# A two-layer hybrid encoder: the opening, the last pair of each ConvFFN and the ending written out by hand

## The chip, the cores and the metric

The kernel runs on one core of a Trainium2 chip. The metric is the device time of one execution in microseconds, smaller is better.

The core has TensorE (PE, the matrix products, with its weight loads as PEld), VectorE (DVE), ScalarE (ACT), GpSimd (POOL) and SyncE (SP). Each runs its own queue of instructions in order. SyncE issues DMAs; GpSimd can issue them too, from its own queue, among its other instructions.

## The reference

The kernel computes one step of a two-layer encoder on 1024 prompt frames and 32 frames of a running stream, with 1024 channels:

```
rmsnorm(x, g) = x * rsqrt(mean(x*x) + 1e-6) * g

layer 0:  gb, gc, u = split(rmsnorm(x, a_norm) @ w_in, 3)     # short gated conv
          x = x + (gb * causal_conv3(gc * u)) @ w_out
          x = x + conv_ffn(rmsnorm(x, ffn_norm[0]))
shared:   k, v, forget = rmsnorm(x, kv_norm) @ w_kv
layer 1:  q = rmsnorm(x, b_norm) @ w_q
          x = x + forgetting_attention(q, k, v, forget) @ w_o
          x = x + conv_ffn(rmsnorm(x, ffn_norm[1]))
y = rmsnorm(x, final_norm)

conv_ffn(h):  g, v = split(causal_conv3(h @ w_up), 2)         # 2 x 2816 channels
              return (silu(g) * v) @ w_down
```

The output is y and the new states (the last two rows of each convolution, K, V and the forget logits).

## The kernel before

All activations are kept with channels on partitions. The stream x is eight tiles of 128 channels by 1056 tokens (1024 and 32), x0 to x7. The token axis is cut in three chunks of 352 (`CH`), in two halves of 528 (`HALVES`), or, before a norm, in four chunks of 264 (`ENDS`). A product of float32 numbers is made of three products of a rounded type: each operand is split into a high part (ScalarE copies it into the rounded type) and a low part (VectorE subtracts the high part from the number), and `chain` (L259, L260, L261) adds high by high, low by high and high by low in one bank of PSUM. A weight tile goes the same way: `weights` (L222) loads it raw by SyncE, ScalarE makes wh (L236) and VectorE wl (L237). A unit is the product of all of x with 128 output channels: eight blocks, three chunks and three products, so 72 products.

The order of instructions in each queue is set by a scheduler with a model of times. Where code runs under `strict` (L102), the instructions of TensorE, VectorE and ScalarE keep the order in which they are written, and all are recorded with line 73; SyncE and GpSimd go by the scheduler there too.

**The opening.** `build` loads the eight tiles of x and two weight tiles. `normed` splits each tile, times its gain, into xh (L248) and xl (L249), and squares it on ScalarE (L314); the squares are added to acc by GpSimd, the last by VectorE (L315). The first units do not wait for the statistics of the norm: `start(acc, 2)` makes the first two (gc and u of the mixer) go through `outer`, block by block, and `settle` multiplies their results later by the scale. The scale comes from `rstd`: 24 small products of acc with ones (L359), the square root on ScalarE, a Newton step on VectorE, a diagonal dg, and products of dg with ones (L332) that spread the scale over the partitions. The third unit (gb) goes the usual way, behind the scale.

**The end of ConvFFN.** `ffn` runs over 22 pairs of units g and v. For each pair it puts the two rows of state in front of a sample's tokens (`halo`, L483, GpSimd), copies the last rows out (`tail`, L487, GpSimd), makes the three taps (the first on ScalarE, L497, two on VectorE, L501), silu, product and split (L832, L833). While these loops run, x lies in DRAM; behind them SyncE loads its eight tiles again, 16 DMAs of 128x528 (L165). Then come the last four activations of w_down: in layer 0 by `down`, with weight tiles by `weights`; in layer 1 by blocks of 512 columns (L716, L723, L724) and `tokenwise`.

**The ending.** In layer 1 `tokenwise` goes chunk by chunk of 264 tokens and row by row (m = 0 to 7): 12 products for a row, VectorE adds them to x, ScalarE squares, VectorE adds the square to acc. `tick` moves a counter on by one row, and `at(n, f)` puts f that many rows later. In the first chunk all rows get their first three activations ahead of the last one. The statistics of a chunk stand in the next one (`rstd_steps`). `result` (L455) writes the output of a chunk behind its scale: ScalarE x * gain, GpSimd that times the scale (L468), DMA (L469); in the last chunk VectorE makes six rows at once from x, gain and scale, and ScalarE with GpSimd two.

The tiles x and y lie in a pool of 24 buffers (`keep`), weight tiles in one of four, raw weights in one.

## Time and profile before

| what | us |
|---|---|
| timed runs | 2527.67, 2531.79, 2531.83 |
| their median | 2531.79 |
| the profiled execution | 2527.23 |
| its span, from first to last instruction | 2525.40 |
| busy in it: TensorE | 2462.6 (98%) |
| VectorE | 1525.6 (60%) |
| ScalarE | 1213.8 (48%) |
| GpSimd | 898.5 (36%) |

The profile is of one execution. Its times count from the start of the span. TensorE's granted clock is given as a share of full speed; the mean over the span is 0.994. A row of the timeline gives in brackets how long the engine stood idle ahead of the instruction, and what released it.

### The profile page before, as it was taken

How to read it: one execution, taken by the hardware profiler on the slowest of the kernel's cores; microseconds unless marked ns; L12 is line 12 of the kernel's file. 1: busy time of each engine (PE TensorE's matmuls, PEld its weight loads, DVE VectorE, ACT ScalarE, POOL GpSimd, SP SyncE). 2: the span in 40 equal slices, each digit the busy share in tenths (PEclk: the TensorE clock that was granted, in tenths of full speed). 3: DMA queues.
4: the chain of work that ended last, by engine and by line, in shares of the span. 5: the costliest groups of instructions: out<-in, count | busy, mean ns of one | idle time of the engine just before them, and what ended most of it. 6: DMA issues, size and time to landing. Idle time of an engine off the chain costs nothing. (4 is left out here: it accounts for less than half of the span.)

```text
span 2525.4 us, 47206 instructions
## 1 busy us (share of the span) xinstructions
PE 2462.6 (98%) x18484; PEld 2425.1 (96%) x18484; DVE 1525.6 (60%) x2593; ACT 1213.8 (48%) x2380; POOL 898.5 (36%) x952
## 2 busy tenths in 40 slices
PE   7999999999999999999999999999999999999997
PEld 7999999999999999998999999999999999999996
DVE  6443448855555555666676667665885555555575
ACT  4111114555555545445666666643554555555544
POOL 3000012444444434342544445412244444334423
PEclk9999999999999999999999999999999999999998
DMA  3111123376666666532322223373246766666751
GB/s 120 42 48 45 49 87 93 65 131 120 119 117 111 119 118 120 138 114 65 80 73 76 76 78 81 81 245 102 71 95 119 128 117 119 114 114 116 123 138 69
DMA packets 147631, 254.76 MB, mean 101 GB/s; under 512 B 22352, under 2 KB 58320, under 8 KB 147408
## 3 DMA queue, kind: packets, MB, share of 16 engines
q0 software_dynamic: 41472, 77.88, 23.2%
q1 hardware_dynamic: 105936, 173.87, 22.9%
q8 instruction: 145, 2.38, 0.4%
q14 instruction: 78, 0.64, 0.1%
HBM read 130.52 MB, written 113.04 MB: 96 GB/s over the span
## 5 line engine op out<-in xcount | busy, mean ns | idle before, releaser
L734 PE MATMUL pb_p<-b,wb 128*128 128x264 f32 x6720 | 894.8, 284 | 2.0 <-ACT u L776 2.0
L734 PEld LDWEIGHTS pb_p<-b,wb 128*128 128x128 f32 x6720 | 850.0, 188 | 2.4 <-ACT u L776 2.4
L900 POOL DMA_DIRECT2D xd<-xs x288 | 262.8, 917 | 495.9 <-ACT xs L898 494.5
L898 ACT ACTIVATE xs<-pb_d 128x264 f32<-128x264 f32 x576 | 218.3, 387 | 349.8 <-PE pb_d L261 307.5
L259 PE MATMUL pb_d<-acth,wb 128*128 128x264 f32 x1152 | 327.7, 285 | 1.3 <-ACT xs L898 1.3
L260 PE MATMUL pb_d<-actl,wb 128*128 128x264 f32 x1152 | 327.5, 285 | 0.0
L261 PE MATMUL pb_d<-acth,wb 128*128 128x264 f32 x1152 | 327.3, 285 | 0.0
L259 PE MATMUL pb_d<-xh,wh 128*128 128x384 f32 (+2 forms) x864 | 283.1, 331 | 8.4 <-ACT xh L248 7.5
L260 PE MATMUL pb_d<-xl,wh 128*128 128x384 f32 (+2 forms) x864 | 282.1, 327 | 5.9 <-DVE xl L249 5.8
L261 PE MATMUL pb_d<-xh,wl 128*128 128x384 f32 (+2 forms) x864 | 281.4, 326 | 0.0
L501 DVE SCALAR_TENSOR_TENSOR y<-u,cv,y 128x1058 f32<-128x1058 f32 x186 | 238.9, 1330 | 54.0 <-ACT y L497 53.9
L259 PEld LDWEIGHTS pb_d<-acth,wb 128*128 128x128 f32 x1152 | 216.6, 188 | 2.2 <-ACT xs L898 1.9
L261 PEld LDWEIGHTS pb_d<-acth,wb 128*128 128x128 f32 x1152 | 216.9, 188 | 0.0
L260 PEld LDWEIGHTS pb_d<-actl,wb 128*128 128x128 f32 x1152 | 216.8, 188 | 0.0
L236 ACT ACTIVATE wh<-wraw 128x1024 fp32r<-128x1024 f32 (+1 forms) x69 | 72.3, 1047 | 258.2 <-PE pb_d L260 137.4
L483 POOL COPY u<-cv 128x4 f32<-128x4 f32 x96 | 64.9, 676 | 346.3 <-DVE u L691 248.7
L724 DVE TENSOR_TENSOR wb<-wr,wb 128x512 fp32r<-128x512 f32 x196 | 153.1, 783 | 55.8 <-ACT wb L723 45.5
L724 DVE TENSOR_TENSOR wb<-ws,wb 128x512 fp32r<-128x512 f32 x160 | 125.0, 783 | 98.0 <-ACT wb L723 98.0
L259 PEld LDWEIGHTS pb_d<-xh,wh 128*128 128x128 f32 x864 | 162.7, 189 | 10.0 <-ACT xh L248 8.2
L756 POOL TENSOR_TENSOR ws<-wr 128x512 f32<-128x512 f32 x80 | 122.3, 1528 | 137.0 <-DMA wr<-in_w_up 113.6
L260 PEld LDWEIGHTS pb_d<-xl,wh 128*128 128x128 f32 x864 | 163.1, 189 | 8.0 <-DVE xl L249 7.7
L261 PEld LDWEIGHTS pb_d<-xh,wl 128*128 128x128 f32 x864 | 162.9, 189 | 0.3
(343 smaller groups left out, 4949.8 us busy)
## 6 DMA issues: line engine op xcount, KB each, us to landing
xd<-xs POOLq DMA_DIRECT2D x288, 264.0 KB, 4.3
wr<-in_w_up SPq DMA_DIRECT2D x168, 256.0 KB
wr<-in_w_down SPq DMA_DIRECT2D x80, 256.0 KB
x<-xd SPq DMA_DIRECT2D x48, 264.0 KB
wraw<-in_w_in SPq DMA_DIRECT2D x23, 512.0 KB
xd<-x SPq DMA_DIRECT2D x64, 132.0 KB
wraw<-in_w_kq SPq DMA_DIRECT2D x16, 512.0 KB
xd<-x SPq DMA_DIRECT2D x16, 264.0 KB
```

Source lines behind the costliest of these rows:

```text
L236: nc.scalar.activation(h[:, i:j], raw[:, i:j], AF.Copy)
L259: nc.tensor.matmul(ps, wh, xh[:, c[0]:c[1]], start=(i == 0), stop=False)
L260: nc.tensor.matmul(ps, wh, xl[:, c[0]:c[1]], start=False, stop=False)
L261: nc.tensor.matmul(ps, wl, xh[:, c[0]:c[1]], start=False, stop=(i == n - 1))
L483: self.nc.gpsimd.tensor_copy(v, st.rearrange("p (a b) -> p a b", b=2))
L501: self.nc.vector.scalar_tensor_tensor(y, u[:, i:i + TC], w[:, i:i + 1], y, op0=OP.mult, op1=OP.add)
L724: nc.vector.tensor_sub(t[:, 1], src, t[:, 0].bitcast(F32))
L734: nc.tensor.matmul(ps[:, q, :QB], w[:, i, k], t[:, j, cs], start=(begin and k == 0 and n == 0), stop=(end and k == len(b) - 1 and n == 2), ...
L756: getattr(self.nc.gpsimd, "tensor_" + op)(dst, x, y)
L898: nc.scalar.activation(t[:, q * QB:(q + 1) * QB], ps, AF.Copy)
L900: nc.gpsimd.dma_start(d, t, accum_op=OP.add)
```

## The change

Three functions are written anew, and all that is in them is put in order by hand under `strict`.

`opening` takes the place of the loads in `build`, of `normed`, `start` and `settle` for the first three units. All loads are issued at the start, with the raw weights of the second unit between x3 and x4 and those of the third behind x7, each in a buffer of its own. ScalarE and VectorE split all of x first; the squares (ScalarE) and their sums (VectorE, none on GpSimd) stand behind that, between the products of the second unit. The statistics stand behind the first chunk of the third unit, the products that spread the scale behind its second.

`halved`, in `ffn`, takes the place of `act` for the last pair: both halo copies first, then taps, silu, product and split for the columns up to 528, and then for the rest. The 16 loads of x go to GpSimd's queue, and in layer 0 the weights of `down` get a high priority.

`ending` takes the place of `tokenwise` with `lag` and of `result`. ScalarE writes x * gain into y right behind the square of the same row, in every chunk. The add of a square to acc comes two rows later (one for the last row). Behind the scale GpSimd multiplies rows 0 to 4 and VectorE rows 5 to 7, which reads the scale from PSUM; in the last chunk VectorE takes rows 0 to 5.

At the start of attention some chains of products change places in TensorE's order, with no code of their own changed; the scheduler sets that.

```
     def load(self, x, m, queue=None):
         x[m] = self.keep(f"x{m}")
         for d, cs in self.spilled(m):
-            self.nc.sync.dma_start(x[m][:, cs], d)
+            (queue or self.nc.sync).dma_start(x[m][:, cs], d)
...
+    def ending(self, weight, acts, x):
...
+        def add(ps, m, c, y):
+            cs = slice(*c)
+            xc = x[m][:, cs]
+            self.nc.vector.tensor_add(xc, xc, ps)
+            sq = acc[:, cs] if m == 0 else self.temp("sq")[:, :c[1] - c[0]]
+            self.nc.scalar.activation(sq, xc, AF.Square)
+            self.nc.scalar.activation(y[m // 2][:, m % 2], xc, AF.Copy, scale=self.gain[:, 5, m:m + 1])
+            if m:
+                self.at(1 if m == NK - 1 else 2, lambda: self.nc.vector.tensor_add(acc[:, cs], acc[:, cs], sq))
+
+        def scaled(y, m, c, r):
+            engine, by = (self.nc.gpsimd, out[:, slice(*c)]) if r is None else (self.nc.vector, r)
+            engine.tensor_mul(y[m // 2][:, m % 2], y[m // 2][:, m % 2], by)
...
             for m in range(NK):
+                ps = early[m] if early else next(banks)[:, :n]
+                self.chain(ps, weight(m), acts, c, range(g - 1, g) if early else None)
+                self.tick()
+                self.at(1, lambda ps=ps, m=m, c=c, y=y: add(ps, m, c, y))
...
+        for m in (0, 6, 1, 2, 7, 3, 4, 5):
+            scaled(y, m, c, None if m > 5 else r)
...
-                tiles[i // 8] = self.weights(units[i // 8])
+                with self.tc.high_priority(offset=2 * AHEAD) if lag else nullcontext():
+                    tiles[i // 8] = self.weights(units[i // 8])
...
+    def opening(self, x, gain):
...
+        products(0, range(1))
+        for m in range(1, NK):
+            high(m)
+            low(m)
+            if m == 1:
+                whigh(0, 2)
+                wlow(0, 2)
+            products(0, range(m, m + 1))
+        whigh(1)
+        wlow(1)
+        sq = [self.slot("sq") for _ in range(NK)]
+        for m in range(NK):
+            ACT.activation(sq[m], x[m], AF.Square)
+            if m:
+                DVE.tensor_add(sq[0], sq[0], sq[m])
+            products(1, range(m, m + 1))
+            if m == 1:
+                for i in range(3):
+                    evict(0, i)
+            if m == 4:
+                whigh(2)
+                wlow(2)
...
+        def halved(t, g, v):
...
+            for u, _, i in both:
+                self.halo(u, st[:, i])
...
+            for a, b in ((0, HB), (HB, TC)):
...
-            put_off += act(t, *us)
+            put_off += act(t, *us) if t < NF - 1 else [lambda: halved(t, *us)]
...
         for m in range(NK):
-            self.load(x, m)
+            self.load(x, m, nc.gpsimd)
...
-                self.tokenwise(lambda m: [(ws[m][:, 0, k], ws[m][:, 1, k]) for k in range(4)], acts, x,
-                               self.result(x), lag=True)
+                self.ending(lambda m: [(ws[m][:, 0, k], ws[m][:, 1, k]) for k in range(4)], acts, x)
```

VectorE at the opening, before (wraw is a raw weight tile, wh and wl its parts, x_99 to x_106 the blocks of x, sq a square):

```order
L237 TENSOR_TENSOR wl<-wraw,wh 128x256
L237 TENSOR_TENSOR wl<-wraw,wh 128x768
L249 SCALAR_TENSOR_TENSOR xl<-x_99,gain,xh 128x352 x3
L249 SCALAR_TENSOR_TENSOR xl<-x_100,gain,xh 128x1056
L249 SCALAR_TENSOR_TENSOR xl<-x_101,gain,xh 128x1056
L249 SCALAR_TENSOR_TENSOR xl<-x_102,gain,xh 128x1056
L249 SCALAR_TENSOR_TENSOR xl<-x_103,gain,xh 128x1056
L237 TENSOR_TENSOR wl<-wraw,wh 128x1024
```

The same place after (wr is the raw tile of `opening`):

```order
L73 TENSOR_TENSOR wl<-wr,wh 128x256
L73 SCALAR_TENSOR_TENSOR xl<-x_99,gain,xh 128x352 x3
L73 SCALAR_TENSOR_TENSOR xl<-x_100,gain,xh 128x1056
L73 TENSOR_TENSOR wl<-wr,wh 128x768
L73 SCALAR_TENSOR_TENSOR xl<-x_101,gain,xh 128x1056
L73 SCALAR_TENSOR_TENSOR xl<-x_102,gain,xh 128x1056
L73 SCALAR_TENSOR_TENSOR xl<-x_103,gain,xh 128x1056
L73 SCALAR_TENSOR_TENSOR xl<-x_104,gain,xh 128x1056
L73 SCALAR_TENSOR_TENSOR xl<-x_105,gain,xh 128x1056
L73 SCALAR_TENSOR_TENSOR xl<-x_106,gain,xh 128x1056
L73 TENSOR_TENSOR wl<-wr,wh 128x1024
L73 TENSOR_TENSOR sq<-sq 128x1056
```

The rest of the first weight's low part stands behind block 1 now, the second weight's behind all blocks, and the sums of squares, which GpSimd made beside these rows, follow there on VectorE.

GpSimd at the end of ConvFFN in layer 0, before (u is the output of a unit, cv the states, ws a weight block that GpSimd adds up):

```order
L756 TENSOR_TENSOR ws<-wr,ws 128x512
L483 COPY u<-cv 128x2x2 x2
L487 COPY cv<-u 128x4 x2
L483 COPY u<-cv 128x2x2 x2
L487 COPY cv<-u 128x4
```

The same place after (xd is x in DRAM; the first two and the last two of the 16 loads are shown):

```order
L909 TENSOR_TENSOR ws<-wr,ws 128x512
L512 COPY u<-cv 128x2x2 x2
L516 COPY cv<-u 128x4
L165 DMA x_11708<-xd_69 128x528
L165 DMA x_11708<-xd_70 128x528
...
L165 DMA x_11729<-xd_83 128x528
L165 DMA x_11729<-xd_84 128x528
L516 COPY cv<-u 128x4
L512 COPY u<-cv 128x2x2 x2
L516 COPY cv<-u 128x4
```

The 16 loads stand ahead of the tail copy of the pair before and of the two halo copies of the last pair.

ScalarE in the last chunk of the ending, before (ne is the square root in the statistics, the numbered x are rows 0 to 7):

```order
L73 ACTIVATE sq<-x_28324 128x264
L73 ACTIVATE y<-x_28309,gain 128x264
L73 ACTIVATE y<-x_28312,gain 128x264
L73 ACTIVATE y<-x_28315,gain 128x264
L73 ACTIVATE y<-x_28318,gain 128x264
L73 ACTIVATE y<-x_28321,gain 128x264
L73 ACTIVATE y<-x_28324,gain 128x264
L73 ACTIVATE sq<-x_28327 128x264
L73 ACTIVATE y<-x_28327,gain 128x264
L73 ACTIVATE y<-x_28330,gain 128x264
L73 ACTIVATE sq<-x_28330 128x264
L73 ACTIVATE ne<-pb_d,epst 88x3
```

The same place after:

```order
L73 ACTIVATE sq<-x_28344 128x264
L73 ACTIVATE y<-x_28344,gain 128x264
L73 ACTIVATE sq<-x_28347 128x264
L73 ACTIVATE y<-x_28347,gain 128x264
L73 ACTIVATE sq<-x_28350 128x264
L73 ACTIVATE y<-x_28350,gain 128x264
L73 ACTIVATE sq<-x_28353 128x264
L73 ACTIVATE y<-x_28353,gain 128x264
L73 ACTIVATE ne<-pb_d,epst 88x3
```

Before, six writes of y of the chunk ahead stand between the squares of rows 5 and 6; after, each square is followed by the write of its own row.

## Rows read from the trace of the kernel before

**Rows 1.** Stretches from the span's start, TensorE: us, busy (instructions), clock, DMA share, GB/s.

```profile
0.00:56.77 56.77, 42.64 (x247) 1.00 0.36 124
56.77:350.00 293.23, 293.23 (x1841) 1.00 0.16 47
...
1050.00:1250.00 200.00, 191.22 (x1254) 0.98 0.33 100
...
2448.00:2525.40 77.40, 56.84 (x422) 0.86 0.25 90
```

**Rows 2.** Timeline of the opening: start, us, engine, line, operation, count [idle <-releaser].

```profile
8.95 0.49 PE L261 MATMUL pb_d<-xh,wl 128*128 128x352 f32 x1
...
9.24 0.49 PE L259 MATMUL pb_d<-xh,wh 128*128 128x352 f32 x1
...
9.73 1.18 ACT L248 ACTIVATE xh<-x,gain 128x1056 fp32r<-128x1056 f32 x1 [0.37 <-DMA x<-in_x]
...
10.94 1.32 DVE L249 SCALAR_TENSOR_TENSOR xl<-x,gain,xh 128x1056 fp32r<-128x1056 f32 x1 [1.52 <-ACT xh L248]
...
11.96 19.78 POOL L315 TENSOR_TENSOR acc<-acc,sq 128x1056 f32<-128x1056 f32 x6 [10.66 <-ACT sq L314]
...
12.98 9.58 DVE L249 SCALAR_TENSOR_TENSOR xl<-x,gain,xh 128x1056 fp32r<-128x1056 f32 x3 [0.72 <-ACT xh L248]
...
15.74 0.43 PE L260 MATMUL pb_d<-xl,wh 128*128 128x352 f32 x1 [1.63 <-DVE xl L249]
```

**Rows 3.** Timeline of TensorE at the statistics of the opening.

```profile
45.23 1.97 PE L359 MATMUL pb_o<-ones,acc 128*88 128x1 f32 x24
...
53.05 1.94 PE L332 MATMUL pb_d<-dg,ones 88*128 88x352 f32 x6
```

**Rows 4.** Timeline at the end of ConvFFN in layer 0.

```profile
1055.29 8.61 SPq L165 DMA_DIRECT2D x<-xd  x16
...
1077.28 0.19 POOL L483 COPY u<-cv 128x4 f32<-128x4 f32 x1 [4.57 <-DVE u L807]
...
1078.72 5.02 DVE L501 SCALAR_TENSOR_TENSOR y<-u,cv,y 128x1058 f32<-128x1058 f32 x4 [1.47 <-ACT y L497]
...
1084.92 0.43 PE L261 MATMUL pb_p<-acth,wl 128*128 128x352 f32 x1 [2.00 <-DVE wl L237]
...
1087.18 0.43 PE L259 MATMUL pb_p<-acth,wh 128*128 128x352 f32 x1 [0.87 <-ACT acth L832]
```

**Rows 5.** Instructions of line 900 on GpSimd: count, ns min/median/max, first and last start.

```profile
L900 POOL DMA_DIRECT2D xd<-xs x288: 852/865/2151, 485.3 to 2417.3; - x144
```

**Rows 6.** Timeline from the end of ConvFFN in layer 1 to the end.

```profile
2430.22 0.18 POOL L487 COPY cv<-u 128x4 f32<-128x4 f32 x1
...
2449.68 0.19 POOL L483 COPY u<-cv 128x4 f32<-128x4 f32 x1 [2.40 <-DVE u L807]
...
2455.68 0.39 PE L73 MATMUL pb_p<-acth,wb 128*128 128x264 f32 x1 [1.52 <-ACT wb L723]
...
2461.28 0.28 PE L73 MATMUL pb_p<-acth,wb 128*128 128x264 f32 x1
...
2465.54 0.42 ACT L73 ACTIVATE sq<-x 128x264 f32<-128x264 f32 x1 [0.84 <-DVE x L73]
...
2471.71 0.63 PE L73 MATMUL pb_d<-ones,acc 128*88 128x1 f32 x6 [1.91 <-DVE acc L73]
...
2507.64 2.53 ACT L73 ACTIVATE y<-x,gain 128x264 f32<-128x264 f32 x6
...
2508.37 0.43 DVE L73 TENSOR_TENSOR x<-x,pb_p 128x264 f32<-128x264 f32 x1 [0.17 <-PE pb_p L73]
...
2510.51 0.84 DVE L73 TENSOR_TENSOR acc<-acc,sq 128x264 f32<-128x264 f32 x1 [1.71 <-ACT sq L73]
...
2517.59 3.51 DVE L73 SCALAR_TENSOR_TENSOR y<-x,gain,rstd 128x264 f32<-128x264 f32 x6 [1.89 <-ACT rstd L73]
```

**Rows 7.** One stretch of the ending, TensorE: columns as in rows 1.

```profile
2471.71:2508.33 36.62, 35.69 (x276) 0.95 0.17 61
```

More of the change, by code (lines that the diff above doesn't have):

```diff
@@ L1 @@
[L1 removed]
+from contextlib import ExitStack, contextmanager, nullcontext
 from itertools import zip_longest
@@ L385, in tokenwise @@
+    def tokenwise(self, weight, acts, x, scale, units):
+        g = len(acts)
+        banks = self.singles(self.spare())
         acc, out = self.keep("acc"), self.keep("rstd")
@@ L396, in tokenwise @@
             cs, n = slice(*c), c[1] - c[0]
-            early = [next(wide)[:, :n] for _ in range(NK)] if lag and c is ENDS[0] else []
-            for m, ps in enumerate(early):
-                self.chain(ps, weight(m), acts, c, range(g - 1))
             if c is ENDS[-1]:
@@ L453, in f @@
             return [lambda m=m: one(m, c, r) for m in range(NK)]
-        return f
-    def result(self, x):
-        per = 2
-        def some(m, c, r):
-            nc, cs, n = self.nc, slice(*c), c[1] - c[0]
-            y = self.keep("y", [128, per, n])
-            for i in range(per):
-                gain = self.gain[:, 5, m + i:m + i + 1]
-                if c is ENDS[-1] and m + per < NK:
-                    nc.vector.scalar_tensor_tensor(y[:, i], x[m + i][:, cs], gain, r, op0=OP.mult, op1=OP.mult)
-                else:
-                    nc.scalar.activation(y[:, i], x[m + i][:, cs], AF.Copy, scale=gain)
-                    nc.gpsimd.tensor_mul(y[:, i], y[:, i], r)
-            nc.sync.dma_start(self.a["o_y"][m:m + per, :, cs].rearrange("m p c -> p m c"), y)
-        def f(c, r):
-            return [lambda m=m: some(m, c, r) for m in range(0, NK, per)]
         return f
@@ L1408, in build @@
     x = [net.keep(f"x{m}") for m in range(NK)]
[L1409 to L1421 removed]
+    with net.phase(SLOTS):
+        net.fresh = 0
+        with net.strict():
+            opened = net.opening(x, 0)
+        net.mixer(x, *opened, net.normalise(x, 1))
     with net.phase(UPSLOTS, banks=UPBANKS):
```

194 lines of the change are left out of this document (154 added, 40 removed).

## The prediction

> **What bounds the kernel now.** [...] What can be won lies where TensorE has gaps: 14.1 us of the first 56.77, 8.8 us of the 200 around the start of attention, and 20.6 us of the last 77.40. The same rows give the price of a product: 293.23 / 1841 = 0.159 us at 352 columns, or 0.122 at 264 by the ratio of columns (in the ending 35.69 / 276 = 0.129 at a clock of 0.95, which is 0.123 at 1.00 [rows 7]). Then I read the timeline of the three places in time order and asked of every gap which engine ended it.
>
> **The opening.** Before: TensorE needs 9 products for a block of x (three chunks, three products each), 9 x 0.159 = 1.43 us. The low half of one block costs VectorE 1.32 us as long as GpSimd is still (start 10.94), but 9.58 / 3 = 3.19 us each from 12.98 on, while GpSimd adds squares at 19.78 / 6 = 3.30 us each [rows 2]. TensorE then waits at each block for the low half, 1.63 us at 15.74; the weights of the second unit fill part of that. So VectorE, slowed beside GpSimd, sets the pace. After: GpSimd adds nothing here; VectorE makes all low halves first and adds the squares behind them. The cost by steps: block 1 has its high half at 9.73 + 1.18 = 10.9 and its low half at 12.2, as before. Then comes the rest of the first weight's low half, three quarters of such a tile, estimated at 0.96 from the 1.32 of 1056 columns, and the low half of block 2: 12.2 + 0.96 + 1.32 = 14.5. Of that block 8 products are left, 8 x 0.159, so 15.8. Behind it VectorE needs 1.32 and ScalarE 1.18 a block against TensorE's 1.43, so TensorE sets the pace: five blocks, 7.15, end at 23.0. Units two and three are 144 products, 22.9, end 45.9. The statistics cost TensorE 1.97 (24 small products) and 1.94 (6 more) [rows 3], and the chain from them to the scale now has the third unit's chunks beside it: 49.8, where the fourth unit starts, instead of 56.77 (the end of the first window [rows 1]). That is **-7.0**. The squares that VectorE now adds (seven, 1.32 each, 9.2 us) and the squares, weights and evictions on ScalarE lie beside the 22.9 us of units two and three; without that cover they would cost up to 9.2. Better end: -7.5, if half of the 0.96 is hidden. [...]
>
> **The end of ConvFFN in layer 0.** TensorE idles 2.00 us for the low half of the second w_down tile, which VectorE takes only behind four whole taps of 5.02 us, then 0.87 us for the last activation's high half [rows 4]: 2.87 in all. After: that tile stands ahead of the taps on VectorE, and the last pair goes in two halves. A tap costs 1.25 whole, so some 0.63 in half; by the four half taps, the silu, the product and the split, counted from the halo copy at 1077.28, the first half of the activation has its high part at about 1084.2, where the whole one came at 1087.18, and its low part at 1085.7. TensorE still waits for these, some 0.7 us: about 2.2 of the 2.87 are won, I take **-2.1**. Ends: -0.5 (the halves cost their fixed price twice on ScalarE and VectorE, which eats the gain) and -2.8 (nearly all of the gap).
>
> **The 16 loads of x on GpSimd.** They move from SyncE's queue to GpSimd's, ahead of the two halo copies of the last pair, so the taps wait behind them: this is the step that can cost. In layer 0 they can be issued from 1055.29, when SyncE issued them, and the second halo copy runs at 1077.28 [rows 4]: 21.9 us for 16, or 1.37 us each. In layer 1 GpSimd is at that place at 2430.22, and the halo follows at 2449.68 [rows 6]: 19.5 us, or 1.22 each. This kernel shows what GpSimd pays for issuing a DMA of the same 128x528: 0.865 us in the median of 144, at most 2.151 [rows 5]. 16 x 0.865 = 13.8 fits in both, so the price is **0**; above 1.2 to 1.4 us it is paid on the path to the end. In return SyncE's queue is free in layer 1 for the w_down tiles, which is counted below.
> [...]
>
> **The start of attention.** Some chains of scores and value products change places; no work is added. TensorE idles 8.78 of 200 us there [rows 1], 2.87 of it at the place just priced. I take **0**, with -2 and +2 as ends: a third of the remaining 5.9 either way.
>
> **The ending.** Three things change (times on the clock of the old trace). First, the w_down tiles no longer queue behind the loads of x: TensorE waited until 2455.68 for one, 1.52 us [rows 6], and started again at the lower level, so that the products with the last activation began at 2461.28; without the wait and the slow products I expect about 2458.6. Second, ScalarE now writes y right behind each square and the add of the square comes two products later. Before, a square of the first chunk started only every 1.27 us with ScalarE idle 0.84 us for x [rows 6], because add, square and add followed each other on VectorE and ScalarE; so the column sums came at 2471.71, with TensorE idle. Now ScalarE's two passes, 2 x 0.42, set the pace: 2458.6, some 1.2 until the first square, 8 x 0.84 = 6.7, which gives 2466.5. Third, from there to the last product TensorE needed 36.62 us, at a granted clock of 0.95 [rows 7]. 276 products and sums at 0.122 and a little more are 34.2 at the full level, and I add 1.1 for the loading of the square-root table, which now stands in ScalarE's way: 35.3 to 36.8, depending on the level. So the last product is at 2501.8 to 2503.3, I take 2502.5 instead of 2508.33: -5.8. The tail behind it was 2525.40 - 2508.33 = 17.07 us. In it VectorE waits 1.71 us for a square [rows 6], because six writes of y (2.53 us) stand ahead of the last squares on ScalarE; that is gone. Behind the scale VectorE spends 3.51 us on six products from SBUF; now six that read the scale from PSUM, as the add at 2508.37 reads PSUM in 0.43, 2.6, and without waiting for the copy of the scale (about 0.9). 1.7 + 0.9 + 0.9 = -3.5. Ending in all **-9.3**. Ends: -3.8, when only the weight's wait (2.1 with the slow products) and the 1.71 go; -12, when the level stays full, the table's load is hidden (2466.5 + 34.2, so -7.6) and the tail loses 0.8 more on GpSimd's two late products.
>
> **Sum.** -7.0 - 2.1 + 0 - 9.3 = -18.4. The profiled execution took 2527.23 (span 2525.40 and 1.83 outside), so 2508.8 on its own scale. It lies 4.6 below the median of the three timed runs (2531.79); the mean of all four is 2529.63, and I set the forecast from that: 2511. Bounds added up: -7.5 - 2.8 - 2 - 12 = -24.3 gives 2505; -3.5 - 0.5 + 2 - 3.8 = -5.8 gives 2524.
>
> **Rivals.** (1) The ending is not shortened by its inner rhythm: ScalarE with two passes per row, or the wait for y's buffers behind their transfers, becomes the bound. For it: ScalarE gets 16 passes into a chunk that TensorE does in 8 x 12 x 0.122 = 11.7 us; that is 6.7, so against it. Price: only -3.8 there, -12.9 in all, 2517. [...] (3) Slower than before: GpSimd's queue jams. At the largest price of [rows 5], 2.151 us, 16 loads are 34.4 us; the halo of layer 0 comes 12.5 late and that of layer 1 14.9 late, and nothing on TensorE covers it, since the last activation is what it waits for. -18.4 + 27.4 = +9.0, 2539. This turns the sign from (41.4 + 18.4) / 32 = 1.87 us per load; between 1.7 and 2.0 the two cancel to within 0.2%. For it: VectorE is busy with two-operand work all along there, and GpSimd doubled VectorE's price in the opening [rows 2]. Against it: 0.865 is the median of 144.
>
> **How the numbers follow.** Forecast 0.60 (2505 to 2516), rival 1 0.17, rival 2 0.08, the jam 0.07, in between 0.08. All but the last two lie inside 2505 to 2524, 0.85. A measurement of this kernel can tell some 0.2% (5 us) from no change. Faster 0.60 + 0.17 + 0.08 = 0.85, same 0.08, slower 0.07.
>
> **What would show it.** Opening: the low halves at 1.3 us each, no wait of TensorE for them after the second block, and the fourth unit's first product near 49.8. Layer 0: last activation's first product near 1084 and gaps of about 1 us; GpSimd's 16 loads under 1 us each and the halo copies not later than before. Ending: no wait for a w_down tile, the first column sums at 2466.5 less the 9.1 won ahead of it, 2457.4, and some 13.5 us from the last product to the end. It is wrong if a halo copy starts right behind a load, if the granted clock of the first 25 us or the last 70 is lower than before, or if attention's 200 us grow by over 2.

## The result and the profile after

The changed kernel takes 2516.02 us (median of 4 runs, 2515.19 to 2516.51) against 2531.54 before (4 runs): a ratio of 0.9942, interval 0.9925 to 0.9959, or 15.5 us less. In a second measurement it took 2515.80 (5 runs) against 2530.14 (15 runs): 0.9944, 0.9931 to 0.9958. The forecast was 2511.0, with 2505 to 2524 as the range: the direction and the range hold, the gain of 18.4 that the sum gives was 3 to 4 us too large.

The profiled execution after has a span of 2513.9 us, the first one before 2525.40 us. Where the 11.5 us between these two lie is read from the start of the same instruction in both. Times are us from the start of the span; the third column is a second profile of the kernel before, which was taken later and has its place among the experiments.

| place | before | before, second | after |
|---|---|---|---|
| first product of the fourth unit | 56.77 [rows 1] | 56.42 | 50.92 |
| the 2161st product, at the end of the mixer | 364.52 | 364.06 | 360.59 |
| GpSimd's copy ahead of the loads of x in layer 1 | 2430.22 [rows 6] | 2432.97 | 2427.73 |
| first column sums of the ending | 2471.71 [rows 6] | 2474.66 | 2464.01 |
| last product | 2508.05 | 2510.34 | 2498.19 |
| end of the span | 2525.40 | 2527.7 | 2513.9 |

**The opening.** The timeline after (start, us, engine, line, operation, count, idle and releaser):

```profile
12.13 0.66 PE L73 MATMUL pb_d<-xl,wh 128*128 128x352 f32 x1 [0.69 <-DVE xl L73]
...
14.69 2.49 ACT L73 ACTIVATE xh<-x,gain 128x1056 fp32r<-128x1056 f32 x2 [1.10 <-DMA x<-in_x]
...
15.90 5.25 DVE L73 SCALAR_TENSOR_TENSOR xl<-x,gain,xh 128x1056 fp32r<-128x1056 f32 x4 [0.50 <-ACT xh L73]
...
39.50 1.97 PE L73 MATMUL pb_s<-ones,sq 128*88 128x1 f32 x24
```

The low halves now cost 5.25 / 4 = 1.31 us each, where they cost 3.19 [rows 2]. TensorE waits for the last time at 12.13. The product there takes 0.66 us against 0.32 later; those behind it start 0.29 us apart, and from 16.34 on 0.16. The statistics start at 39.50 instead of 45.23 [rows 3]. The stretch behind it (stretch, us, busy with count, granted clock, DMA share, GB/s):

```profile
16.23:50.92 34.69, 34.69 (x225) 1.00 0.22 76
```

From 16.23 on TensorE has no gap: 225 instructions in 34.69 us. The granted clock reads 1.00 for the stretch ahead of it too (0.00:16.23), but its first record in the trace begins at 16.23; before the change it begins at 12.51.

The first profile is one of ten with this opening: nine more stand among the experiments, in kernels that differ from the changed one only behind it or, in the opening alone, have only this of it. In these ten the clock's first record (1.00) begins, and the slow products end, between 14.69 and 18.38 us, and the fourth unit starts between 49.93 and 52.00, the later, to within 0.2 us, the later that is.

**The end of the mixer.** Here the gain of 5.85 shrinks to 3.93. Before, and then after, in two stretches each, and the waits after:

```profile
346.00:353.80 7.80, 5.88 (x47) 1.00 0.24 68
353.80:357.30 3.50, 3.50 (x16) 0.51 0.51 150
```

```profile
346.00:354.10 8.10, 3.98 (x27) 1.00 0.22 65
354.10:357.60 3.50, 3.50 (x16) 0.51 0.65 179
```

```profile
346.92 0.39 PE L73 MATMUL pb_d<-acth,wh 128*128 128x264 f32 x1 [1.08 <-ACT wh L236]
...
352.82 0.39 PE L73 MATMUL pb_s<-acth,wh 128*128 128x264 f32 x1 [1.71 <-ACT wh L236]
...
354.08 0.55 PE L73 MATMUL pb_s<-acth,wl 128*128 128x264 f32 x1 [0.74 <-DVE wl L237]
```

In both kernels TensorE waits here for tiles of w_out, two pairs of waits one behind the other, and in both the granted clock drops to 0.50 for 3.41 us. Before, the slow stretch (353.80 to 357.30) lay ahead of the second pair, and of that only 0.75 us was left: the wait became shorter by what the slow products cost. After, the second pair took 1.71 and 0.74 us, and the slow stretch lay behind it, on the path. The first pair is the same in both (1.17 and 0.75, 1.08 and 0.75), and comes 5.54 us earlier after: up to it, nearly all of the gain of the opening is there.

Which of the two cases an execution shows doesn't follow from the change. The second pair of waits in the opening alone, and in the ending alone, which has the old opening:

```profile
353.89 0.39 PE L73 MATMUL pb_s<-acth,wh 128*128 128x264 f32 x1 [0.28 <-ACT wh L236]
355.15 0.39 PE L73 MATMUL pb_s<-acth,wl 128*128 128x264 f32 x1 [0.75 <-DVE wl L237]
```

```profile
358.00 0.39 PE L73 MATMUL pb_s<-acth,wh 128*128 128x264 f32 x1 [1.80 <-ACT wh L236]
359.26 0.59 PE L73 MATMUL pb_s<-acth,wl 128*128 128x264 f32 x1 [0.75 <-DVE wl L237]
```

From the fourth unit's first product to the 2161st it takes 307.6 to 308.1 us where the slow stretch lies ahead of the long wait of the second pair (both profiles of the kernel before and three traces with the new opening) and 309.5 to 310.9 where it begins behind that wait (the ending alone and seven traces with the new opening). The latest of these, with the squares on GpSimd, comes 7.6 us after the kernel before and loses about as much (309.5) as the changed kernel (309.7).

**ConvFFN in layer 0.** The rows that answer to [rows 4]:

```profile
1051.64 5.47 POOL L165 DMA_DIRECT2D x<-xd  x10
...
1073.23 1.22 DVE L237 TENSOR_TENSOR wl<-wraw,wh 128x1024 fp32r<-128x1024 f32 x1
...
1073.35 1.15 POOL L512 COPY u<-cv 128x4 f32<-128x4 f32 x1 [4.56 <-DVE u L960]
...
1081.50 0.43 PE L259 MATMUL pb_p<-acth,wh 128*128 128x352 f32 x1 [1.38 <-ACT acth L1011]
...
1082.94 0.43 PE L260 MATMUL pb_p<-actl,wh 128*128 128x352 f32 x1 [0.69 <-DVE actl L1012]
```

GpSimd issues ten loads in 5.47 us, 0.55 each, the last of the 16 at 1060.89, long before the halo copy at 1073.35. The wait for the second w_down tile, 2.00 us [rows 4], is gone. The waits for the last activation are 1.38 and 0.69, instead of 0.87 and 0.18. The halo copy itself takes 1.15 us here, where it took 0.19 [rows 4]: it starts 0.12 us behind VectorE's low half of that w_down tile and ends with it.

**The ending.**

```profile
2427.92 5.46 POOL L165 DMA_DIRECT2D x<-xd  x10
...
2447.58 0.62 POOL L512 COPY u<-cv 128x4 f32<-128x4 f32 x1 [2.80 <-DVE u L960]
...
2464.01 0.63 PE L73 MATMUL pb_d<-ones,acc 128*88 128x1 f32 x6
...
2500.94 0.84 PE L73 MATMUL pb_d<-ones,acc 128*88 128x1 f32 x6 [2.47 <-DVE acc L73]
...
2505.20 2.13 DVE L73 TENSOR_TENSOR y<-y,pb_d 128x264 f32<-128x264 f32 x6 [1.82 <-ACT rstd L73]
```

There is no wait for a w_down tile any more. From the copy ahead of the loads to the column sums it takes 2464.01 - 2427.73 = 36.28 us instead of 41.49; from there to the last product 34.18 instead of 36.34, without the low clock that [rows 7] shows (it reads 1.00 from 2464.01 to 2498.33; the second profile of the kernel before has none there either, and takes 35.68); from there to the end 15.7 instead of 17.35.

**The end of the span.** Before and after, the rows of the last line of the program (count, ns min/median/max, first and last start):

```profile
L1509 POOLq DRAIN  x3: 40/93/5393, 2518.3 to 2525.2; - x3
L1509 SPq DRAIN  x3: 7/7/7, 2524.6 to 2524.9; - x3
```

```profile
L1677 POOLq DRAIN  x3: 40/93/7891, 2505.3 to 2513.6; - x3
L1677 SPq DRAIN  x3: 7/7/7, 2511.1 to 2513.4; - x3
```

The last line of the program holds a drain for each engine. SyncE reaches its own at 2511.1 after, but the first drain of GpSimd, which starts at 2505.3 and takes 7.89 us, ends at 2513.1, and the program with it. Before, GpSimd's took 5.39 and ended at 2523.7, ahead of SyncE's at 2524.6. So 2.0 us are lost here that no row of the kernel before pointed to.

A drain is recorded from before GpSimd's last product ends, so its length says little by itself (after, it starts at 2505.3, and the product ends at 2506.68). From the end of that product to the end of the drain it takes 6.46 us after (to 2513.14) and 4.14 before (2519.60 to 2523.74). Over all traces it is 4.13 or 4.14 in the six with the loads of x on SyncE, with the old ending and with the new, and 6.46 in the seven with the 32 loads on GpSimd.

### The profile page after: what moved, and what is told of

Same layout as the page of the kernel before. It is cut to its first block, busy times and chain, and to the rows that moved or that the text cites. A ratio compares the mean times of both kernels' runs of the same rounds, so it can differ in the third digit from the quotient of the medians.

```text
span 2513.9 us, 47244 instructions
## 1 busy us (share of the span) xinstructions
PE 2462.6 (98%) x18484; PEld 2425.7 (96%) x18484; DVE 1527.3 (61%) x2622; ACT 1217.8 (48%) x2394; POOL 892.2 (35%) x969
## 5 line engine op out<-in xcount | busy, mean ns | idle before, releaser
L259 PE MATMUL pb_d<-xh,wh 128*128 128x384 f32 (+2 forms) x816 | 269.2, 330 | 0.8 <-DVE x L562 0.7
L260 PE MATMUL pb_d<-xl,wh 128*128 128x384 f32 (+2 forms) x816 | 266.2, 326 | 0.0
L261 PE MATMUL pb_d<-xh,wl 128*128 128x384 f32 (+2 forms) x816 | 266.0, 326 | 0.0
L530 DVE SCALAR_TENSOR_TENSOR y<-u,cv,y 128x1058 f32<-128x1058 f32 x178 | 228.8, 1329 | 53.0 <-ACT y L526 52.9
L236 ACT ACTIVATE wh<-wraw 128x1024 fp32r<-128x1024 f32 x65 | 68.9, 1060 | 265.6 <-PE pb_o L260 125.4
L259 PEld LDWEIGHTS pb_d<-xh,wh 128*128 128x128 f32 x816 | 154.1, 189 | 1.8 <-issue 1.0
L876 ACT ACTIVATE wb<-wr 128x512 fp32r<-128x512 f32 x196 | 123.4, 630 | 66.5 <-PE pb_p L887 58.1
L260 PEld LDWEIGHTS pb_d<-xl,wh 128*128 128x128 f32 x816 | 154.2, 189 | 0.4
```

What stands on the lines that cost most here:

```text
L236: nc.scalar.activation(h[:, i:j], raw[:, i:j], AF.Copy)
L259: nc.tensor.matmul(ps, wh, xh[:, c[0]:c[1]], start=(i == 0), stop=False)
L260: nc.tensor.matmul(ps, wh, xl[:, c[0]:c[1]], start=False, stop=False)
L261: nc.tensor.matmul(ps, wl, xh[:, c[0]:c[1]], start=False, stop=(i == n - 1))
L530: self.nc.vector.scalar_tensor_tensor(y, u[:, i:i + TC], w[:, i:i + 1], y, op0=OP.mult, op1=OP.add)
L876: nc.scalar.activation(t[:, 0], src, AF.Copy)
```

## The experiments

The letters in the expectations: theory A, each term of the sum stands by itself as the prediction sized it; B, the next wait or the next drop of the clock takes part of a gain back; C, the stretches at the lower clock differ from one execution to the next; D, GpSimd's drain ends the program; E, the loads have room in GpSimd's queue; F, one raw buffer sets the end of the mixer.

### The opening alone

The kernel before, with `opening` in place of its loads and first units, and nothing else of the change.

> The kernel before with the new opening alone. Theory A (each part's gain stands by itself): the fourth unit starts near 50.9 us instead of 56.77, and the whole is 5.9 us below the kernel before, near 2525.6. Theory B (the gain of one place is partly given back where TensorE's granted clock next falls or where the next wait for a weight tile ends): the fourth unit starts at 50.9 all the same, but by 365 us only 4 are left, and the whole is 3 to 4 us below, near 2528.

Measured: 2524.74 us (11 runs, 2523.43 to 2528.28) against 2529.97 before, ratio 0.9978 (0.9969 to 0.9987): 5.2 us. In its trace the fourth unit starts at 52.00, 4.8 us earlier than before and not at 50.9 as both theories had it (the slow products ended at 18.38), and at the 2161st product 4.4 are left. The time lies between the two theories: the opening is worth about five us by itself, and the loss at the end of the mixer is smaller here than in the changed kernel's trace (0.4 against 1.9), since the slow stretch lies ahead of the second pair of waits.

### The ending alone

The kernel before with `ending`; loads of x in SyncE's queue, the last pair whole.

> The kernel before with the new ending alone; the loads of x stay in SyncE's queue, ahead of the w_down tiles of the ending. Theory A (the ending's own rhythm and tail carry most of its 9.9 us, the wait for the w_down tile the rest): TensorE still waits 1.5 us for the tile near 2455.7, and the whole is 6 to 7 us below the kernel before, near 2525. Rival (the rhythm is worth nothing by itself, the loads' move carries it): under 3 us below, 2529 or more.

Measured: 2522.85 us (5 runs, 2518.31 to 2525.03), ratio 0.9966 (0.9954 to 0.9979): 7.1 us, near theory A's 6 to 7. The waits of TensorE from 2440 us on (engine, line, releaser: us in all, times, longest):

```profile
PE pb_p L73 <- DVE wb L753: 1.1, 1, 1.1
PE pb_p L73 <- ACT wb L752: 1.0, 1, 1.0
```

The two waits for the w_down tile (1.1 and 1.0) are there, which the changed kernel doesn't have. This trace shows something else too. Up to the loads of x in layer 1 its instructions are those of the kernel before; yet GpSimd's copy there starts at 2437.49, against 2430.22 and 2432.97 in the two profiles of that kernel. Up to seven us lie between executions of the same instructions, and a part of them is the lower clock: between 1220 and 1250 us it is 0.89 here and 1.00 in the first profile of the kernel before (more on this with its second profile, below), and 2.7 come at the end of the mixer, as shown above.

### The loads of x back on SyncE

```
-            self.load(x, m, nc.gpsimd)
+            self.load(x, m)
```

> The changed kernel with the 16 loads of x of both layers back in SyncE's queue. Theory A: the w_down tile is late again in layer 1, 2 to 3 us are lost there, 2518 to 2519; as the scheduler then sets the start of attention in the old order, up to 2 us may come back, so 2516.5 to 2519. Rival (GpSimd's queue delays the halo copies, so the old queue was the better): 2514 or less.

Measured: 2513.59 us (5 runs, 2512.16 to 2515.95), ratio 0.9936 (0.9923 to 0.9950). Theory A fell: without the move the kernel is not slower (nor shown to be faster: the interval overlaps that of the changed kernel, 0.9925 to 0.9959). The w_down waits came back in its trace (0.96 and 1.17 us), but GpSimd's drain is 5.57 us again and no longer last. So in these traces the move wins the wait for the tiles and pays 2.0 us of it back at the end. The two can't be told apart by this run alone: its profile also loses nothing at the start of attention, where that of the changed kernel loses 2.3; the next two runs take them apart. The rival's reason, halo copies that wait for the loads, is not what the trace shows. The halo copy of layer 0 is short here all the same:

```profile
1072.85 0.19 POOL L512 COPY u<-cv 128x4 f32<-128x4 f32 x1 [4.56 <-DVE u L960]
```

In this kernel and the next the scheduler puts VectorE's low half of the second w_down tile behind the taps of the first half. The first high part then comes 7.1 us behind the start of the copy instead of 8.1, but the low half delays the rest: over the end of ConvFFN (products 7400 to 8200) TensorE takes 110.5 us either way.

### The loads on SyncE, behind the w_down tiles

```
-        for m in range(NK):
-            self.load(x, m, nc.gpsimd)
...
             ws = [self.operand(self.block(u, i), n % 2) for n, u in enumerate(units) for i in range(2)]
+            for m in range(NK):
+                self.load(x, m)
```

In layer 0 the loads stand where they stood, on SyncE.

> The changed kernel with the loads of x back in SyncE's queue, in layer 1 behind the eight w_down tiles instead of ahead of them. Theory D (of the move to GpSimd only the free way for the w_down tiles is of use, and GpSimd's last drain, 7.9 us with the loads on it and 5.4 to 5.6 without, costs 2 us at the end): no wait for a w_down tile, the drain 5.5 us, 2 us below the changed kernel, near 2513. Rival (x now lands too late for the first adds): above the changed kernel.

Measured: 2512.89 us (5 runs, 2512.54 to 2515.36), ratio 0.9937 (0.9925 to 0.9950), against 2515.80 for the changed kernel in the same measurement. The drain:

```profile
L1679 POOLq DRAIN  x3: 40/162/5570, 2503.9 to 2510.7; - x3
```

No wait for a w_down tile is left in its trace, and x lands in time. The 2.9 us are a little more than the 2 expected, with one slow stretch fewer at the start of attention, one more in the ending and a longer one at the end of the mixer. The runs overlap with those of the changed kernel (2513.92 to 2516.39), so the times alone don't show the gain; the end of the span does, 13.4 us behind the last product instead of 15.7.

### GpSimd's last products moved away

```
-        for m in (0, 6, 1, 2, 7, 3, 4, 5):
-            scaled(y, m, c, None if m > 5 else r)
+        for m in range(NK):
+            scaled(y, m, c, r)
```

> The changed kernel with all eight products of the last chunk by the scale on VectorE, so that GpSimd's last work is some 8 us earlier. Theory D (GpSimd's drain is what ends the program): the drain begins earlier and is hidden; VectorE's two more products cost 0.7 us, and the end comes 1.3 us earlier, so 1 to 1.5 us below the changed kernel. Rival (the drain only waits for what the others do): 0.7 us above it.

Measured: 2512.52 us (5 runs, 2511.65 to 2513.71), ratio 0.9934 (0.9922 to 0.9946), 3.3 below the changed kernel of the same measurement, whose fastest run (2513.92) is above the slowest here.

```profile
L1677 POOLq DRAIN  x3: 40/93/10037, 2492.9 to 2509.6; - x3
```

```profile
2503.18 2.81 DVE L73 TENSOR_TENSOR y<-y,pb_d 128x264 f32<-128x264 f32 x8 [1.82 <-ACT rstd L73]
```

GpSimd's drain starts at 2492.9 now, ends at 2503.0 and is hidden (its 10.04 us hold GpSimd's products of the chunk before; from the end of the last it is 6.46 again); all drains are done at 2509.6. VectorE needs 2.81 us for eight products, 0.68 more than for six. From the last product to the end it takes 2.0 us less, which is theory D; the other 2.0 between the two traces lie ahead of the ending, most of them at the start of attention, where this one has no slow stretch between 1220 and 1250 us.

### The last pair in one piece

```
-            put_off += act(t, *us) if t < NF - 1 else [lambda: halved(t, *us)]
+            put_off += act(t, *us)
```

> The changed kernel with the last pair of each ConvFFN in one piece. Theory A: TensorE waits longer for the last activation, 1.5 us in layer 0 and about 1 in layer 1, 2518 to 2519. Rival (two halves cost their fixed price twice and give back what they win): within 0.5 us of 2516.

Measured: 2518.66 us (5 runs, 2517.64 to 2522.03), ratio 0.9956 (0.9943 to 0.9968), some 3 us above the changed kernel (0.9942 and 0.9944, with intervals that overlap this one). Layer 0, waits of TensorE and the granted clock without the halves and with them:

```profile
PE pb_p L259 <- ACT acth L985: 3.1, 1, 3.1
PE pb_p L260 <- DVE actl L986: 0.2, 1, 0.2
...
1060.00:1100.00 40.00, 36.67 (x235) 0.96 0.37 127
2430.00:2470.00 40.00, 37.21 (x295) 0.96 0.39 138
```

```profile
PE pb_p L259 <- ACT acth L1011: 1.4, 1, 1.4
PE pb_p L260 <- DVE actl L1012: 0.7, 1, 0.7
...
1060.00:1100.00 40.00, 37.92 (x254) 1.00 0.41 140
2430.00:2470.00 40.00, 38.26 (x310) 1.00 0.37 135
```

The wait for the whole activation is 3.1 + 0.2 us against 1.4 + 0.7, and the same in layer 1 (1.9 + 0.9 against 0.3 + 1.0). Behind the longer wait the granted clock falls as well, to 0.96 in both stretches: by estimate 40 x 0.04 = 1.6 us more. Halving won 1.2 and 1.5 us of waiting. The drop of the clock behind it can't be put down to the whole pair: the kernel with all last products on VectorE has the halves and the same two waits in layer 0 (1.4 and 0.7), and its clock falls from 1082.72 to 1086.13 all the same.

### The squares of the opening on GpSimd again

```
+            ACT.activation(sq[m], x[m], AF.Square)
+            nc.gpsimd.tensor_add(sq[0], sq[0], sq[m])
...
-            ACT.activation(sq[m], x[m], AF.Square)
-            if m:
-                DVE.tensor_add(sq[0], sq[0], sq[m])
```

The added lines stand right behind the split of each block.

> The changed kernel, with the squares of the opening made between the splits again and added by GpSimd, as before the change. Theory A (the low halves are slow beside GpSimd's adds, and this is what the opening wins): low halves of 3.2 us each, TensorE waits 1.6 us at each block, the fourth unit starts 4 to 6 us later than at 50.9, and the whole is 3 to 6 us above the changed kernel. Rival (the order by hand and the early weights carry the gain): within 1.5 us of the changed kernel.

Measured: 2528.40 us (10 runs, 2524.88 to 2529.90), ratio 0.9994 (0.9985 to 1.0003): all of the change's gain is gone, 12.6 us.

```profile
14.96 20.01 POOL L779 TENSOR_TENSOR sq<-sq 128x1056 f32<-128x1056 f32 x6 [0.23 <-ACT sq L73]
...
15.47 20.61 DVE L73 SCALAR_TENSOR_TENSOR xl<-x,gain,xh 128x1056 fp32r<-128x1056 f32 x6
...
PE pb_d L73 <- DVE xl L73: 10.4, 7, 3.5
```

The low halves take 20.61 / 6 = 3.43 us each while GpSimd adds, against 1.31; the one that started ahead of the first add took 1.32. This is the reason that the prediction gave, shown by one edit (it also puts the squares on ScalarE between the splits, but TensorE's waits of up to 3.5 us are for the low halves). Both engines go at about the same pace there, 3.43 and 20.01 / 6 = 3.34 us. This costs more than the opening had won. TensorE waits for the last of these low halves at 36.14 us, where the changed kernel's last wait is at 12.13. A likely reason, which no run takes apart, is that the order by hand has no products of the second unit between them to fill the waits with, which the kernel before had.

### The add of a square one row behind it

```
-                self.at(1 if m == NK - 1 else 2, lambda: self.nc.vector.tensor_add(acc[:, cs], acc[:, cs], sq))
+                self.at(1, lambda: self.nc.vector.tensor_add(acc[:, cs], acc[:, cs], sq))
```

> The changed kernel with the add of each square to acc one row after it, as before the change, instead of two. Theory A (add, square and add wait for each other in the first chunk of the ending, 1.27 us a row against 0.72): the first column sums come 3 to 4 us later, and the whole is 2 to 4 us above the changed kernel. Rival (ScalarE's passes set the pace either way): within 1 us.

Measured: 2520.09 us (4 runs, 2519.37 to 2522.64), ratio 0.9961 (0.9946 to 0.9976), some 4 us above the changed kernel, in times whose intervals still overlap.

```profile
2459.16 0.43 ACT L73 ACTIVATE sq<-x 128x264 f32<-128x264 f32 x1 [0.43 <-DVE x L73]
...
2460.43 0.42 ACT L73 ACTIVATE sq<-x 128x264 f32<-128x264 f32 x1 [0.43 <-DVE x L73]
...
2465.39 1.04 PE L73 MATMUL pb_d<-ones,acc 128*88 128x1 f32 x6 [1.95 <-DVE acc L73]
```

A square every 1.27 us, as before [rows 6], though ScalarE writes y in between; the changed kernel has 0.72 (from its seven squares between 2458.76 and 2463.08). TensorE waits 1.95 us for the column sums again, and they come 39.9 us behind GpSimd's copy instead of 36.3: 3.6 of the 5.2 us that were won up to there. So the two rows of delay carry most of the gain of the first chunk, and not the place of y; the rest is about the size of the wait for a w_down tile (1.52 [rows 6]). Behind the sums this trace has a slow stretch from 2465.34 to 2472.17, and 2.4 us more up to the last product.

### More DMAs in GpSimd's queue

```
             self.load(x, m, nc.gpsimd)
+            for j in range(2):
+                for i in range(2):
+                    nc.gpsimd.dma_start(self.dr.tile([128, HB], F32, name=f"xe{l}{m}{i}{j}"), self.xd[m][i])
```

> The changed kernel, with 32 more DMAs of the same size in GpSimd's queue behind each layer's 16 loads of x (copies of x in DRAM to a place that nobody reads), so 48 instead of 16 ahead of the halo copies. Theory E (a DMA costs GpSimd 0.55 us to issue, and the halo copies have 21 us of room): 48 take 26 to 29 us, the halo copies come 5 to 6 us late in layer 0 and 7 to 8 in layer 1, the whole is 12 to 14 us above the changed kernel, near 2529; and if the last drain of GpSimd grows by 2.4 us for 32 DMAs, it is 12.7 us now and adds up to 5 us. Rival (the queue is emptied by others and the halo copies don't wait): within 2 us of the changed kernel.

Measured: 2526.25 us (10 runs, 2523.31 to 2529.41), ratio 0.9984 (0.9975 to 0.9993), some 10 us above the changed kernel, but not by the way that was meant. The scheduler put the extra copies ahead of the loads, among the stores of the last groups:

```profile
1013.28 0.49 POOL L1054 DMA_DIRECT2D xe<-xd  x1 [3.98 <-DMA xd<-xs]
...
1056.03 5.44 POOL L165 DMA_DIRECT2D x<-xd  x10
...
1077.51 1.15 POOL L512 COPY u<-cv 128x4 f32<-128x4 f32 x1 [5.35 <-DVE u L960]
```

GpSimd stood 3.98 us in front of such a copy, for the store that it reads, with the work of w_up behind it. The halo copy at 1077.51 waited for VectorE and not for the loads. So the point from which the loads would cost, 1.2 to 1.4 us each, was not reached, and stays untried. One thing the run does settle:

```profile
L1680 POOLq DRAIN  x3: 40/93/6432, 2516.5 to 2523.5; - x3
```

With 64 more DMAs on that queue the drain is shorter, 6.43 us instead of 7.89, and 4.99 instead of 6.46 from the end of GpSimd's last product. So it doesn't grow with their number, and theory E's 12.7 fell.

### The changed kernel and the kernel before once more

> The changed kernel once more, beside the next three on one chip. Theory C (stretches at the lower clock come in another number and at other places in each execution, so two profiles of one kernel differ by some us ahead of the ending): about 0.6% below the kernel before, 2514 to 2517, with low stretches at other places than in the first profile of it. Rival (the places follow from the kernel alone): the same stretches at the same times, to 1 us.

> The kernel before, once more, for a second profile. Theory C (an execution differs from the next by where the stretches at the lower clock fall): ahead of the ending the same instructions come 2 to 4 us later than in the first profile, whose execution was the fastest of the kernel before on its chip. Rival (the first profile shows the usual execution): within 0.5 us of it at every place.

The changed kernel (2515.80, see above) showed its slow stretches at the same places as in its first profile, to a microsecond, against theory C. The kernel before, 2529.52 us in this one execution, did not. Nor do the kernels with the same opening agree: up to the end of the mixer they run the same instructions on TensorE in the same order, and their first slow stretch there starts anywhere from 348.85 to 355.04 us. The same stretch in the first profile of the kernel before, in its second, and in the changed kernel's first:

```profile
1220.00:1250.00 30.00, 28.71 (x190) 1.00 0.29 70
```

```profile
1220.00:1250.00 30.00, 28.89 (x177) 0.89 0.28 70
```

```profile
1220.00:1250.00 30.00, 28.76 (x191) 0.94 0.26 68
```

Between 1220 and 1250 us the first profile has a clock of 1.00, the second 0.89, the changed kernel 0.94. The second profile falls 2.5 us behind the first in this stretch. The profile on which the prediction rested was thus a good execution of the kernel before, and 2.3 us (2527.7 - 2525.4) of the difference between 11.5 (the two first profiles) and 15.5 (the medians) are explained by it.

### A version with the raw tiles in buffers of their own

The kernel with GpSimd's last products moved away, and:

```
-        ws = [self.weights(u, keep=i > 1) for i, u in enumerate(units)]
+        ws = [self.weights(u, keep=i > 1, raw=self.slot("wr", [128, NK, 128]) if own and i > 1 else None)
+              for i, u in enumerate(units)]
```

`weights` uses the given buffer in place of its only one, and the mixer asks for it with `own`.

> The changed kernel with all eight last products by the scale on VectorE, and in the mixer's last group the raw data of two of the four w_out tiles in buffers of their own, so that their loads start before the raw tile ahead of them is used up. Theory F (TensorE's waits of 1.1, 0.7, 1.7 and 0.7 us near 347 to 354 are for that one raw buffer, and the lower clock behind them costs 1.7 more): these waits are gone, 3 to 5 us below the kernel with the eight products alone, near 2508 to 2509. Rival (the lower clock comes at another place instead, and the next wait takes over): 1 us or less.

Measured: 2505.60 us (4 runs, 2503.25 to 2509.08), ratio 0.9905 (0.9889 to 0.9922): 25 us below the kernel before, and faster than the changed one.

```profile
340.00:353.00 13.00, 13.00 (x108) 1.00 0.36 115
353.00:358.00 5.00, 5.00 (x45) 1.00 0.23 81
```

At the end of the mixer TensorE has no gap and no slow stretch. Against the trace of the kernel with the eight products alone, the same product comes 5.7 us earlier behind this place, and 7.1 at the end. That is more than the 3 to 5 expected. In the other trace the gaps there sum to 2.8 us, and the slow stretch of 3.41 costs 1.7 by estimate; the remaining 1.2 have not been traced.

## Why the prediction came out as it did

- **The opening, -7.0.** Measured -5.85 in the trace (50.92 instead of 49.8 for the fourth unit; 49.93 to 52.00 over ten traces), 5.2 in the times. The mechanism is shown by the squares on GpSimd: 3.43 us for a low half beside its adds, 1.31 without. The mis-sized step is TensorE's pace up to the end of block 2, which the sum puts at 15.8 with products 0.159 us apart (293.23 / 1841 [rows 1]): until 16.23 they were 0.29 us apart, and one block of x came 1.10 us late (14.69). No run shows the -3.5 that the bounds take for this place: over the ten traces the fourth unit comes 4.8 to 6.8 us earlier than the 56.77 of the first profile before. In these traces the slow products end within 3.7 us of each other and the fourth unit starts within 2.1; by estimate 3.7 us of them lose 3.7 x (0.29 - 0.16) / 0.29 = 1.7, most of the 2.1, which speaks for them as the main part. One of its signs of being wrong, a lower granted clock in the first 25 us, can't be read from that clock, which reads 1.00 before and after; the slow products did last longer, to 16.23 us instead of 12.51.
- **Between the opening and ConvFFN, 0.** Measured +1.9 against the first profile. The sum had no term for this place. It is not a price of coming earlier: the waits for w_out tiles came as much earlier as everything else, and whether the slow stretch lies ahead of the long one (no loss) or behind it (1.3 to 3.3 us more) differs among executions with the old opening and with the new. So this term is chance as far as the runs show. The version with raw buffers of their own shows that the waits themselves, in both kernels, were there to be removed.
- **ConvFFN in layer 0, -2.1.** Measured -1.2. The w_down tile came in time, as said. The step that was too low is the way to the halved activation: its first high part came 8.1 us behind the start of the halo copy and not 6.9, and TensorE waits 1.38 and 0.69 instead of some 0.7. Of these 1.2 us, 1.0 is the halo copy, which took 1.15 beside VectorE's low half of the w_down tile instead of 0.19: the sum put that low half ahead of the taps at no cost. The rest is the taps, 4.85 / 7 = 0.69 us for a half and not 0.63. With the low half behind the taps it costs the same elsewhere. Against the whole pair, halving wins 2.7 us of waiting over both layers, and some 3 in the times.
- **The loads on GpSimd, 0.** At the halo copies it is 0, as priced, and with more room: 0.55 us each and not 0.865. Line 900, which gave the price, adds while it stores (it stands for 288 stores, not 144); the plain load is cheaper. Hence the jam (rival 3) did not come. All 32 loads took 0.546 to 0.616 us to issue, with taps, sums and products of two tiles on VectorE beside them. But the move has a price that no term had: behind GpSimd's last product its drain takes 6.46 us with it and 4.14 without, and 2.0 of that ends the program. Moving GpSimd's last two products to VectorE wins these 2.0 back.
- **The start of attention, 0.** Against the first profile of the kernel before it is +2.3, of which 1.5 come between 1220 and 1250 us, where the first profile has a clock of 1.00. Against the second, which has 0.89 there with the old order, nothing is lost: the changed kernel is 5.0 us ahead in front of attention, 4.4 at 1220 us and 5.4 behind. Over all traces the same 400 products (8601 to 9000) take 65.1 to 69.6 us in the old order (eight traces) and 65.9 to 68.7 in the new (five). So the new order of the chains is not shown to cost anything, though the prediction had named a growth of over 2 us as a sign of being wrong: by one profile before, that sign can't be read.
- **The ending, -9.3.** Measured -9.0, but with other parts. Up to the column sums -5.2, the very number of the sum (2466.5 on the old clock), but by two errors that cancel: the first square came 0.7 us later than taken (2458.02, or 2460.5 on the old clock, and not 2459.8; the lower level that the sum takes out ahead of it is a clock of 0.50 from 2456.45 to 2459.86 in the trace before, and 1.00 from 2455 to 2464 after), and the rows followed each other at 0.72 us and not 0.84. To the last product -2.2 where -0.6 was taken: two waits for sums of squares of 0.47 and 0.46 us are gone and one of 0.43 is new, and the slow stretch at a clock of 0.50, which costs 3.41 x 0.50 = 1.7, was missing, as in the second profile of the kernel before. The price was too high there too: 0.122 us a product at 264 columns is not the ratio of columns, which gives 0.119, and most follow each other at 0.1175; no run shows the 1.1 for the square-root table: its load takes 1.28 us before (2472.47) as after (2465.18), and shows at most as that wait of 0.43. The tail -1.6 where -3.5 was taken: the last sums come 2.3 earlier and the products cost 1.4 less, but the wait for ScalarE's copy of the scale stays (1.82 us, though the products read PSUM), and from the end of the products to the end of the span it takes 2.3 more, 2.0 of them for GpSimd's drain.
- **The rivals.** The first, an ending not shortened by its inner rhythm, did not come: with the add one row behind its square the old 1.27 us a row return and cost 3.6 us up to the column sums. Of rival 2, the clock, with its chance of 0.08: the slow products of the opening cost about 1 us by estimate, and in the ending the granted clock reads 1.00 (2464.01 to 2498.33) and not 0.95 [rows 7]. The jam did not come.
- **Sum.** In the order of the program, with attention in two parts (its start, and from there to the ending): against the first profile of the kernel before -5.9 + 1.9 - 1.2 + 2.3 + 0.4 - 9.0 = -11.5, against the second -5.5 + 1.8 - 1.2 - 0.5 + 0.1 - 8.6 = -13.9, where the spans give 11.5 and 13.8. The medians differ by 14.3 to 15.5. That the total came so near the forecast is in part luck: the 2.0 us of the drain and the slow stretches, worth one to three us each, were in no term, and some of the latter fell in its favour (in the ending) and some against it (in the mixer).

What stays open: what sets the length of GpSimd's drain behind its last product, 4.14 us without plain loads on its queue, 6.46 with 32 and 4.99 with 96; and what decides, in executions of the same instructions, where the slow stretches fall.

## What to carry to other kernels

When a stage is made faster, look also at the waits that stand behind it and that no term prices: the two pairs of waits at the end of the mixer, for weight tiles with a single raw buffer, were worth as much (5.7 us) as the whole new opening. Price the end of the program by every queue that has to finish, and not by the last transfer alone; an engine with a long drain (here GpSimd, 6.46 us) should get its last work early. When an instruction is moved ahead on one engine, ask what it runs beside on the others: a low half put ahead of the taps made a copy of 0.19 us into one of 1.15. Take a second profile before the sum is made: two executions of one kernel differed here by what single terms were worth, and a loss that looked like the change's own came in executions without it.

## What was not expected of the hardware

- GpSimd's drain at the end: from the end of its last product 4.13 or 4.14 us in six traces of kernels whose plain loads of x are on SyncE, 6.46 in seven with 32 of them on GpSimd, 4.99 with 96.
- A load of 128x528 costs GpSimd 0.55 us to issue; the store with addition of the same size 0.865.
- VectorE's operation on two tiles of 128x1056 took 3.43 us beside GpSimd's adds, and 1.31 alone, a factor of 2.6. A copy of 128x4 on GpSimd took 0.19 us alone and 1.15 when it started 0.12 us behind such an operation of VectorE, with which it ended.
- Gaps of TensorE were often followed by a stretch of 3.41 or 6.83 us at a granted clock of 0.50, but not always by the same: at the end of the mixer it began at 348.85 to 355.04 us with the same instructions, ahead of a wait or behind it (without the gaps at 346 to 354 us there was none); behind gaps of 1.4 and 0.7 us at the end of ConvFFN in layer 0 the clock stayed at 1.00 in the changed kernel's first trace and fell in one with all last products on VectorE.
